# Layer 1's vector sums in other PSUM banks, and another order of splits, norms and squares at three joints of a two-layer backbone

## The chip, the cores and the metric

One core of a Trainium2 chip runs the kernel. The metric is the device time of one execution in microseconds (us); before and after are compared by the medians of several executions. The engines are TensorE (PE, matrix products; PEld is its weight load), VectorE (DVE), ScalarE (ACT), GpSimd (POOL) and SyncE (SP), whose queue issues the transfers here. Each engine works through its own instructions in order and waits on semaphores for the others. PSUM, into which PE writes, has 8 banks of 512 columns.

## The reference, cut to what matters

Two layers over 1024 latent tokens and 256 context tokens of width 1024. Layer 0 mixes tokens by windowed means, layer 1 by attention (8 query heads, 2 key heads of width 128, keys of latent and context tokens). Both end in a gated FFN of width 2816 with a convolution over three positions. Ahead of each part stand an RMS norm and a shift and scale that come from a vector c.

```python
for i in range(DEPTH):
    sh1, sc1, g1, sh2, sc2, g2 = split(silu_c @ ada_w[i] + ada_b[i], 6)
    h = _modulate(_rmsnorm(x, norm_w[i, 0]), sh1, sc1)
    ...
    y = _pool_mixer(...) if i == 0 else _attention_mixer(...)
    x = x + g1 * y
    x = x + g2 * _conv_ffn(_modulate(_rmsnorm(x, norm_w[i, 1]), sh2, sc2), ...)
# attention: q, k = _rmsnorm(q) * q_gain, _rmsnorm(k) * k_gain; rotary on latent q, k;
# p = softmax(q k^T / sqrt(128)); o = p v
```

## The kernel before, in words

All products are done in three passes: every operand is split into a rounded high half, cast by ACT, and a low half, the difference, by POOL or DVE (`split`, L161; the cast is L162, the difference L163; the three matmuls are L166 to L168). Tokens are in ten tiles of 128, 0 to 7 latent, 8 and 9 context.

**Order.** The head of the kernel (layer 0's mixer and the start of its FFN) is put in order by the framework's planner, by its own costs: the code gives instructions in an order of priority (`on`). Where the FFN's first plain product ends, the kernel switches to the order of the program (L874). From there `play` (L567) walks through a list of PE's pieces with their planned duration (T3 = 0.648 us for three matmuls of 512 columns) and issues every other step when its due time is reached. The attention loop is written out by hand, step by step.

**Head.** `mix_out` (L440) takes a mixer product out of PSUM on DVE (L442) and adds it to the tokens on POOL (L443). `norm2` (L482) multiplies a tile by its reciprocal root mean square, on ACT (L484) or DVE (L486). `turn_h2` (L790) transposes the normed tiles on PE (L794) into banks 1, 3 and 5, and DVE and ACT (L800 to L805) make features of them. Before, tiles 0 to 3 are normed on DVE, as steps due in the first microsecond of the FFN's list.

**Layer 0's down projection.** 22 steps of the context part come first, each with a weight row of 512 KB and 128 KB of units, then seven products of sums. `d0_load` (L939) issues the loads four steps ahead, `d0_split` (L952) splits them. `sums0_acts` (L899) loads two operands, makes four sums on DVE (L589, L592) and stores them; the last two of 22 such sums are done beside the context part, due at its start + 8 and + 23. `ada_load` (L1020) fetches rows of layer 1's modulation weights, at times in the list `at_` (L1298).

**Layer 1's tiles.** For each latent tile: V and K (`project(i, 2)`), transposes of the next tile (`prep_b`, L1141: L1111 and L1119, then a split), Q in two halves, and the turn of K (`turn_k`, L1226, transposes L1229). `shape_qk` (L1172) norms Q or K in three parts: square on ACT (L1180) and reduction on DVE (L1181); reciprocal root (L174 to L178) and multiplications (L1186 on DVE, gain L1189 on POOL for Q and on DVE for K); rotation (`rope_ops`, L1195: L1210 to L1214, POOL or DVE).

**Attention.** A score of one head takes two and a half banks, 0 to 2 or 2 to 4, in turn. `soft_max` (L1368) reads it on DVE (L1371), `soft_exp` on ACT (L1376), `soft_div` takes the reciprocal on DVE (L1380) and divides on POOL (L1381). `turn_p` (L1385) transposes probabilities (L1389) into bank 5 or 6 in turn and splits them; `pv` multiplies into bank 7. Per pair of tile and key head there are 10 steps; scores are made at steps 7, 0, 2 and 5. Beside it POOL adds up modulation vectors 3, 4 and 5 of layer 1; `ada_reduce` (L1056) then sums each over partitions on PE (L1064), copies it (L1066), turns it into columns (`ada_cols`, L1047: L323, L1051), and sends the last one out as a row (`to_row`, L302: L305). Its banks before are those of `turn_p`, 5 and 6.

Of the kernel before, what the change touches and what calls it, by code (L numbers as in the profile page):

```python
# [20 lines left out]
KT = D // P  # L21
# [61 lines left out]
def backbone(ctx: ExitStack, tc: tile.TileContext, io, out: bass.AP):  # L83
# [77 lines left out]
    def split(hi, lo, src, lo_eng=None):  # L161
        nc.scalar.copy(hi, src)  # L162
        (lo_eng or nc.gpsimd).tensor_tensor(out=lo, in0=src, in1=hi.bitcast(F32), op=ALU.subtract)  # L163
# [22 lines left out]
    def on(t, *fns):  # L186

        for fn in fns:
            todo.append((t, len(todo), fn))
# [171 lines left out]
    def rstd_of(a, b):  # L361
        rstd_from(ss[:, a:b], D, mm_[:, a:b], rs[:, a:b], tt_[:, a:b])
# [119 lines left out]
    def norm2(i, on_act=False):  # L482
        if on_act:
            nc.scalar.activation(xh2[i], tm(i), AF.Copy, scale=rs[:, i : i + 1])  # L484
        else:
            nc.vector.tensor_scalar(out=xh2[i], in0=tm(i), scalar1=rs[:, i : i + 1], scalar2=None, op0=ALU.mult)  # L486
# [60 lines left out]
    on(71.5, lambda: rstd_of(8, 10))  # L547
    on(71.6, lambda: norm2(8, True), lambda: norm2(9, True))
    on(73, lambda: rstd_of(0, 4))

    h2 = {0: (at(0, KT, 512, r=True), at(16, KT, 512, r=True)),

# [316 lines left out]
    order += [(last, p) for p in (1, 6, 2, "Ga", "Gb", 5, 7, "Va", "Vb", 3, 4)]  # L869
    for j, p in order:  # L870
        put(step0(j, p), j, p)
    acts = [(0.1 + 0.3 * i, lambda i=i: norm2(i)) for i in range(4)] + [(1, lambda: rstd_of(4, NLT))] + [(2, lambda i=i: norm2(i, i > 5)) for i in range(4, NLT)]

    acts += [(t_man, lambda: ctx.enter_context(tc.manual_schedule()))]  # L874
    acts += [(t_lat + 0.01 * q, lambda q=q: t0_subs(q)) for q in range(HK)]
# [265 lines left out]
    def prep_b(i, hf, pt, on_act=False):  # L1141
        turn_half(i, 1, 0, hf, xh_of(i), xf_, pt, on_act)
        if hf:
            split(*h1s[i % 2], xf_.rearrange("p (k t) -> p k t", k=KT), None if i else nc.vector)

    def prep_items(i, banks, on_act=False):
        return [(0.45, lambda hf=hf: prep_b(i, hf, banks(), on_act)) for hf in range(2)]
# [3 lines left out]
    def project(i, cg, bank_=None):  # L1151

        hh, hlo = h1s[i % 2]
        wh, wl = wq[cg]
        qk = qks[i % 2]
        ps = []

        def mm(k):
            if not k:
                ps.append(mmb() if bank_ is None else bank_)  # L1160
            mm3(ps[0], hh[:, k], hlo[:, k], wh[:, k], wl[:, k], k == 0, k == KT - 1)

        def evac():
            if cg < 2:
                nc.scalar.copy(qk[:, 4 * cg : 4 * cg + 4].rearrange("p h d -> p (h d)"), ps[0])
            else:
                nc.scalar.copy(qk[:, HEADS:NH].rearrange("p h d -> p (h d)"), ps[0][:, 0:256])
                nc.scalar.copy(vlat[:, i] if i < NLT else vc[:, i - NLT], ps[0][:, 256:512])

        return [(T3, lambda k=k: mm(k)) for k in range(KT)] + [(0, evac)]  # L1170
# [48 lines left out]
    def turn_q(i, banks, halves=(0, 1)):  # L1219
        for hf in halves:  # L1220
            pt = banks()
            for q in range(4):
                nc.tensor.transpose(pt[:, q * P : (q + 1) * P], qks[i % 2][:, 4 * hf + q], ident)
            nc.scalar.copy(tm(i, hf * 512, (hf + 1) * 512), pt)

    def turn_k(i, pt=None):  # L1226
        pt = tp() if pt is None else pt
        for q in range(KVH):
            nc.tensor.transpose(pt[:, q * P : (q + 1) * P], qks[i % 2][:, HEADS + q], ident)  # L1229
        kv_ = pt[:, 0 : KVH * P].rearrange("p (h t) -> p h t", h=KVH)  # L1230
        split(kth[:, :, i * P : (i + 1) * P], ktl[:, :, i * P : (i + 1) * P], kv_, nc.vector)

    nc.vector.tensor_scalar(out=gain[:, 0], in0=gain[:, 0], scalar1=HD ** -0.5, scalar2=None, op0=ALU.mult)
    def shape_acts(i, which, *times):
        return [(t, lambda p=p: shape_qk(i, which, p)) for p, t in enumerate(times[: 3 if i < NLT else 2])]
# [54 lines left out]
            (ndone[4] + 0.05 + 2.2 * a, lambda a=a, lo=lo: d0_out(lo, 0, BANKS0[4][a], True)),  # L1290
        ]

    for n, t in ((NJ - 2, base + 8), (NJ - 1, base + 23)):
        acts += sums0_acts(n, t, t + 11, 0.9, t + 15, [at(o, 2, HC) for o in ((96, 100), (104, 144))[n % 2]])

    row1 = at(108, 256)
    t = ndone["ctx"]
    at_ = [t - 34, t - 26, t - 18, t - 10, t - 3, t + 3, t + 7, t + 11] + [ndone[1] - 8 + 6.5 * m for m in range(KT)]  # L1298
    at_ += [ndone[2] - 14 + 2.6 * m for m in range(6)] + [ndone[2] + 6.1 + 2 * m for m in range(2)]
    acts += [(t, lambda n=n: ada_load(n)) for n, t in enumerate(at_)]  # L1300
    for u, n0, t, gap, b in ((0, 0, ndone["ctx"] + 4, 2.9, 0), (1, 2 * KT, ndone[2] + 6, 2, 2)):
# [17 lines left out]
    for i in range(NLT - 1):  # L1319
        body = project(i, 2)  # L1320
        if i > 1:
            body += [(0.9, lambda i=i: turn_q(i - 2, tp))]
        if i == 0:
            body.insert(5, (0.2, lambda: turn_k(8)))
        if i == 1:
            body.insert(5, (0.2, lambda: turn_k(0)))
        body += prep_items(i + 1, tp) + project(i, 0)
        if i == 0:
            body += [(0.2, lambda: turn_k(9))]
        body += project(i, 1)  # L1330
        acts += [(base + 16, lambda i=i: rope_in(i + 1))]
        acts += shape_acts(i, "k", base + (7.5 if i else 5.45), base + 9.5, base + 10)
        if i + 2 < NLT:
            acts += [(base + 7.2, lambda i=i: prep_a(i + 2)), (base + 10.5, lambda i=i: prep_s(i + 2))]
        end = base + span(body)
        acts += shape_acts(i, "q", *(end + 0.1, end + 1.5, end + (13 if i < NLT - 2 else 14)))
        if i:
            body += [(0.2, lambda i=i: turn_k(i))]
        pe += body
        base += span(body)  # L1340
# [74 lines left out]
    TS, TT = 2.5 * T3, 0.44  # L1415
    i7 = NLT - 1
    p70, p71 = project(i7, 0), project(i7, 1, bank(7))
    pe += project(i7, 2) + [(0.9, lambda: turn_q(i7 - 2, ptb))] + p70 + p71[:5] + [(0.2, lambda: turn_k(i7, ptb()))] + p71[5:]
    ahead = [(0, h) for h in range(NHG)] + [(1, 0), (1, 1)]
    for n, e in enumerate(ahead):  # L1420
        t = span(pe) + TS
        pe += [(TS, lambda e=e: score(*e))]
        acts += [(t - 0.1, lambda e=e: soft_max(*e))]
        if n < 5:
            acts += [(t, lambda e=e: soft_exp(*e)), (t + 2.4, lambda e=e: soft_div(*e))]
    acts += shape_acts(i7, "k", base + 5.3, base + 6.5, base + 7)
    acts += [(base + 6, lambda: q_split(0)), (base + 11.5, lambda: q_split(1)), (base + 16.7, lambda: shape_qk(i7, "q", 0))]
    acts += [(base + 18.5, lambda: v_split(8)), (base + 25, lambda: v_split(0, nc.vector)), (base + 27.5, lambda: v_split(2, nc.vector))]
    pe += [(TT, lambda n=n: turn_p(n)) for n in range(LOOK)]
    play(pe, acts)  # L1430
    osp = [hl(96, KT, P), hl(140, KT, P)]
# [21 lines left out]
    def ada_add(n):  # L1453
        nc.gpsimd.tensor_tensor(out=acc_[3], in0=acc_[3], in1=ada_row1(n), op=ALU.add)
        ada_next(n)

    extra = {}
    slots = [n for n in range(NT, NTOT) if n % NT in (4, 8)]
    for n, t in zip(range(ADA0, len(ada_list)), slots):
        u, k = ada_list[n]  # L1460
        extra.setdefault(t, []).append(ada_ops[u][k])
        if k:
            extra.setdefault(t + 1, []).append(lambda n=n: ada_add(n))
        sums = ada_reduce(u) if k == KT - 1 else ()
        for m, fn in enumerate(sums):
            extra.setdefault(t + 5 + 5 * m, []).append(fn)
    wo_at = {2: 0, 4: 1, 6: 2, 8: 3, 10: 4, 13: 5, 14: 6, 15: 7}
    pend = [ahead[5]]
    side = {n: lambda i=i, hf=hf: turn_q(i, ptb, (hf,)) for n, i, hf in ((0, i7 - 1, 0), (1, i7 - 1, 1), (16, i7, 0), (19, i7, 1))}
# [458 lines left out]
```

## Time and profile before

| | us |
|---|---|
| median of 3 executions | 2224.29 |
| lowest, highest | 2222.72, 2227.51 |
| the profiled execution, its own time | 2228.45 |
| its span, first to last instruction | 2226.3 |
| PE busy | 2151.0 |
| DVE, POOL, ACT busy | 1528.4, 1325.5, 1000.1 |

The profile is of one execution. A wait is told by the line that waited and the line that ended the wait. All positions in time are microseconds from the first instruction. The head reaches to about 160 us, layer 0's down projection goes from about 700 to 980, layer 1's tiles from there to about 1155, attention to about 1540, and then come the output projection and layer 1's FFN.

### The profile page before, as it was taken

The page shows a single profiled execution, that of the slowest core. Times are in us where ns is not written, and L with a number is a line of the kernel's source. Part 1 is how long each engine was busy: PE and PEld are TensorE (multiplying, and loading weights), DVE is VectorE, ACT ScalarE, POOL GpSimd, SP SyncE. Part 2 cuts the span into 40 slices and gives each one's busy share as a digit, 9 for nine tenths or more (in the row PEclk, how much of TensorE's full clock was granted, in tenths as well). Part 3 has the DMA queues.
Part 4 walks back from the last instruction along what each step waited for, and adds up shares of the span by engine and source line. Part 5 has one row for each costly group of instructions (what it writes and reads, how often), then busy time and mean ns, then how long its engine had stood idle before and what let it go on. Part 6 is the DMA issues. An engine that isn't in the chain of part 4 may idle for free.

```text
span 2226.3 us, 30135 instructions
## 1 busy us (share of the span) xinstructions
PE 2151.0 (97%) x10972; PEld 1775.5 (80%) x10972; DVE 1528.4 (69%) x2101; ACT 1000.1 (45%) x1585; POOL 1325.5 (60%) x881
## 2 busy tenths in 40 slices
PE   7989999999999999999998999999999999999999
PEld 5768888888888777887877877778878888888887
DVE  5677777777778567587776666646776666667565
ACT  4354333443335443544446656644433343344442
POOL 0344677666763467663346766735477777774655
PEclk9999999999999999999999999999999999999999
DMA  8843445544457978660000212122145555559775
GB/s 322 292 127 116 140 137 166 174 140 138 161 163 266 341 275 298 219 198 13 33 22 13 74 62 72 48 80 91 58 151 191 190 193 188 188 194 330 250 242 181
DMA packets 213926, 363.77 MB, mean 163 GB/s; under 512 B 15106, under 2 KB 114066, under 8 KB 213778
## 3 DMA queue, kind: packets, MB, share of 16 engines
q1 hardware_dynamic: 213778, 361.85, 48.0%
q8 instruction: 86, 1.41, 0.2%
q14 instruction: 62, 0.51, 0.1%
HBM read 271.86 MB, written 89.93 MB: 163 GB/s over the span
## 4 chain that ended last, share of the span: by engine, by line
PE 75%; DVE 10%; ACT 4%; issue 4%; POOL 3%; DMA 3%; SPq 0%; ACTq 0%; POOLq 0%; DVEq 0%
PE psum L166 23%; PE psum L167 23%; PE psum L168 23%; PE psum L1389 2%; POOL a_512r L163 2%; DVE a L1371 1%; DVE a L1214 1%; DVE a_512r L163 1%; PE psum L315 1%; DMA a<-g_d 1%; ACT a L1376 1%; PE psum L396 1%; DVE a L1119 1%; ACT a_512r L162 1%; DVE hs L1181 1%
## 5 line engine op out<-in xcount | busy, mean ns | idle before, releaser
L163 POOL TENSOR_TENSOR a_512r<-a,a_512r 128x512 fp32r<-128x512 f32 x353 | 530.6, 1514 | 366.9 <-ACT a_512r L162 309.7
L162 ACT CAST a_512r<-a 128x512 fp32r<-128x512 f32 x507 | 294.4, 618 | 375.1 <-POOL a L657 158.2
L166 PE MATMUL psum<-a_2048r,a_512r 128*128 128x256 f32 (+1 forms) x1120 | 399.4, 357 | 4.1 <-DVE psum L1630 2.4
L167 PE MATMUL psum<-a_2048r,a_512r 128*128 128x256 f32 (+1 forms) x1120 | 399.0, 356 | 0.0
L168 PE MATMUL psum<-a_2048r,a_512r 128*128 128x256 f32 (+1 forms) x1120 | 398.3, 356 | 0.0
L163 DVE TENSOR_TENSOR a_512r<-a,a_512r 128x512 fp32r<-128x512 f32 x154 | 183.3, 1199 | 109.2 <-ACT a_512r L162 105.0
L166 PE MATMUL psum<-a_512r 128*128 128x512 f32 x616 | 242.2, 393 | 0.0
L166 PEld LDWEIGHTS psum<-a_2048r,a_512r 128*128 128x128 f32 x1120 | 211.8, 189 | 37.0 <-DVE psum L1630 2.8
L167 PE MATMUL psum<-a_512r 128*128 128x512 f32 x616 | 239.9, 389 | 0.4 <-POOL a_512r L163 0.4
L168 PE MATMUL psum<-a_512r 128*128 128x512 f32 x616 | 239.9, 389 | 0.0
L167 PEld LDWEIGHTS psum<-a_2048r,a_512r 128*128 128x128 f32 x1120 | 211.6, 189 | 31.1 <-issue 0.4
L168 PEld LDWEIGHTS psum<-a_2048r,a_512r 128*128 128x128 f32 x1120 | 211.5, 189 | 30.2
L719 DVE SCALAR_TENSOR_TENSOR a<-psum,conv,a 128x255 f32<-128x255 f32 (+1 forms) x176 | 154.4, 881 | 89.5 <-ACT a L714 86.2
L166 PE MATMUL psum<-a_4096r,a_1024r 128*128 128x512 f32 x408 | 162.0, 397 | 0.0
L168 PE MATMUL psum<-a_4096r,a_1024r 128*128 128x512 f32 x408 | 160.1, 392 | 1.2 <-POOL a_1024r L163 1.2
L167 PE MATMUL psum<-a_4096r,a_1024r 128*128 128x512 f32 x408 | 160.0, 392 | 0.0
L1649 DVE SCALAR_TENSOR_TENSOR a<-psum,conv,a 128x1023 f32<-128x1023 f32 x88 | 112.9, 1283 | 58.9 <-ACT a L1641 57.4
L163 DVE TENSOR_TENSOR a_512r<-psum,a_512r 128x512 fp32r<-128x512 f32 x160 | 109.5, 690 | 51.6 <-ACT a_512r L162 50.3
L166 PEld LDWEIGHTS psum<-a_512r 128*128 128x128 f32 x616 | 115.6, 188 | 29.9 <-issue 5.4
L1381 POOL TENSOR_SCALAR a<-a,stt 128x1280 f32<-128x1280 f32 x64 | 85.8, 1341 | 86.9 <-DVE stt L1380 73.4
L162 ACT CAST a_512r<-psum 128x512 fp32r<-128x512 f32 x160 | 92.1, 583 | 100.9 <-PE psum L1389 100.9
L168 PEld LDWEIGHTS psum<-a_512r 128*128 128x128 f32 x616 | 115.6, 188 | 24.4
(256 smaller groups left out, 4758.2 us busy)
## 6 DMA issues: line engine op xcount, KB each, us to landing
a<-in_ada_w_dram SPq DMA_DIRECT2D x96, 512.0 KB, 5.0
a<-in_ffn_w_up_dram SPq DMA_DIRECT2D x88, 512.0 KB, 6.7
a<-in_ffn_w_down_dram SPq DMA_DIRECT2D x66, 512.0 KB, 6.4
g_d<-a SPq DMA_DIRECT2D x44, 512.0 KB, 2.7
tw_d<-a SPq DMA_DIRECT2D x44, 512.0 KB, 4.4
a<-g_d SPq DMA_DIRECT2D x44, 512.0 KB, 6.5
sg_d<-a SPq DMA_DIRECT2D x44, 512.0 KB, 4.4
a<-tw_d SPq DMA_DIRECT2D x88, 256.0 KB, 4.3
```

The lines of the kernel that those rows point to most:

```text
L162: nc.scalar.copy(hi, src)
L163: (lo_eng or nc.gpsimd).tensor_tensor(out=lo, in0=src, in1=hi.bitcast(F32), op=ALU.subtract)
L166: nc.tensor.matmul(ps, lh, rh, start=first, stop=False, skip_group_check=shared)
L167: nc.tensor.matmul(ps, lh, rl, start=False, stop=False, skip_group_check=shared)
L168: nc.tensor.matmul(ps, ll, rh, start=False, stop=last, skip_group_check=shared)
L315: nc.tensor.matmul(ps[32 * j : 32 * j + 32], c_t[:, k, :], wt[:, j * 256 : (j + 1) * 256], start=k == 0, stop=k == KT - 1, tile_position=( ...
L396: nc.tensor.matmul(ps[:, a - o : b - o], tm(i, kt * P, (kt + 1) * P), scaled[i][:, a + sh : b + sh], start=q == 0, stop=q == len(parts) - ...
L719: nc.vector.scalar_tensor_tensor(out=dst[:, lo:hi], in0=src[:, lo + d : hi + d], scalar=cv[:, t, f : f + 1], in1=dst[:, lo:hi], op0=ALU.mu ...
L1119: nc.vector.tensor_scalar(out=o, in0=pt[:, q * P : (q + 1) * P], scalar1=sc, scalar2=sh, op0=ALU.mult, op1=ALU.add)
L1381: nc.gpsimd.tensor_scalar(out=pb, in0=pb, scalar1=s_[:, 2:3], scalar2=1.0, op0=ALU.mult, op1=ALU.mult)
L1389: nc.tensor.transpose(pt[:, h * P : (h + 1) * P], probs[(4 * u + h) % len(probs)][:, k * P : (k + 1) * P], ident)
L1649: nc.vector.scalar_tensor_tensor(out=c[:, lo:hi], in0=psum[:, o + lo + d : o + hi + d], scalar=cv[:, t, f : f + 1], in1=c[:, lo:hi], op0=A ...
```

## The change

1. The norms of tiles 0 to 3 ahead of layer 0's FFN go from DVE to ACT, and in the order of priority right behind their reciprocal root.
2. The low half of tile 1's features at the start of layer 1 is made on DVE instead of POOL.
3. The last of the 22 sums of layer 0 (loads, four DVE steps, stores) is due 15 later, and the first eight loads of modulation rows 9 to 1 later.
4. K's square of tile 1 is due at 5.45 instead of 7.5.
5. The second part of tile 6's q norm is due 11 after its tile instead of 1.5. K's square of tile 7 stands right behind its projection, ahead of the turn of tile 5's q; its other parts are due 0.9 and 1.3 earlier.
6. At the start of attention, the square of tile 7's q stands behind the first soft max instead of before it; the first piece of V's split behind the fifth soft max and behind the reciprocal for the fourth head, instead of before that; the sixth soft max is due 0.6 later.
7. The sums of modulation vectors 3 to 5 are taken at steps 4, 7 and 9 of a pair, in banks 3, 0 and 3, instead of 5 and 10 (and 15) steps behind the last row in banks 5 and 6.

```diff
     on(73, lambda: rstd_of(0, 4))
+    on(73.1, *(lambda i=i: norm2(i, True) for i in range(4)))
...
-    acts = [(0.1 + 0.3 * i, lambda i=i: norm2(i)) for i in range(4)] + [(1, lambda: rstd_of(4, NLT))] + [(2, lambda i=i: norm2(i, i > 5)) for i in range(4, NLT)]
+    acts = [(1, lambda: rstd_of(4, NLT))] + [(2, lambda i=i: norm2(i, i > 5)) for i in range(4, NLT)]
...
-            split(*h1s[i % 2], xf_.rearrange("p (k t) -> p k t", k=KT), None if i else nc.vector)
+            split(*h1s[i % 2], xf_.rearrange("p (k t) -> p k t", k=KT), nc.vector if i < 2 else None)
...
-    for n, t in ((NJ - 2, base + 8), (NJ - 1, base + 23)):
+    for n, t in ((NJ - 2, base + 8), (NJ - 1, base + 38)):
...
-    at_ = [t - 34, t - 26, t - 18, t - 10, t - 3, t + 3, t + 7, t + 11] + [ndone[1] - 8 + 6.5 * m for m in range(KT)]
+    at_ = [t - 25, t - 18, t - 11, t - 4, t, t + 4, t + 8, t + 12] + [ndone[1] - 8 + 6.5 * m for m in range(KT)]
...
-        acts += shape_acts(i, "k", base + (7.5 if i else 5.45), base + 9.5, base + 10)
+        acts += shape_acts(i, "k", base + (7.5 if i > 1 else 5.45), base + 9.5, base + 10)
...
-        acts += shape_acts(i, "q", *(end + 0.1, end + 1.5, end + (13 if i < NLT - 2 else 14)))
+        acts += shape_acts(i, "q", *((end + 0.1, end + 1.5, end + 13) if i < NLT - 2 else (end + 0.1, end + 11, end + 14)))
...
-    pe += project(i7, 2) + [(0.9, lambda: turn_q(i7 - 2, ptb))] + p70 + p71[:5] + [(0.2, lambda: turn_k(i7, ptb()))] + p71[5:]
+    pe += project(i7, 2) + [(0, lambda: shape_qk(i7, "k", 0)), (0.9, lambda: turn_q(i7 - 2, ptb))] + p70 + p71[:5] + [(0.2, lambda: turn_k(i7, ptb()))] + p71[5:]
...
-        acts += [(t - 0.1, lambda e=e: soft_max(*e))]
+        t0_ = t - 0.1 if n == 0 else t0_
+        acts += [(t + (0.5 if n == 5 else -0.1), lambda e=e: soft_max(*e))]
         if n < 5:
-            acts += [(t, lambda e=e: soft_exp(*e)), (t + 2.4, lambda e=e: soft_div(*e))]
-    acts += shape_acts(i7, "k", base + 5.3, base + 6.5, base + 7)
-    acts += [(base + 6, lambda: q_split(0)), (base + 11.5, lambda: q_split(1)), (base + 16.7, lambda: shape_qk(i7, "q", 0))]
-    acts += [(base + 18.5, lambda: v_split(8)), (base + 25, lambda: v_split(0, nc.vector)), (base + 27.5, lambda: v_split(2, nc.vector))]
+            acts += [(t, lambda e=e: soft_exp(*e)), (t + (1.55 if n == 3 else 2.4), lambda e=e: soft_div(*e))]
+        if n == 4:
+            acts += [(t - 0.03, lambda: v_split(0, nc.vector))]
+    acts += [(base + 5.6, lambda: shape_qk(i7, "k", 1)), (base + 5.7, lambda: shape_qk(i7, "k", 2))]
+    acts += [(base + 6, lambda: q_split(0)), (base + 11.5, lambda: q_split(1)), (t0_ + 0.01, lambda: shape_qk(i7, "q", 0))]
+    acts += [(base + 18.5, lambda: v_split(8)), (base + 27.5, lambda: v_split(2, nc.vector))]
...
+    REST = {4: 3, 7: 0, 9: 3}
     extra = {}
...
-        sums = ada_reduce(u) if k == KT - 1 else ()
-        for m, fn in enumerate(sums):
-            extra.setdefault(t + 5 + 5 * m, []).append(fn)
+        t += 2
+        for fn in ada_reduce(u) if k == KT - 1 else ():
+            while t % NT not in REST:
+                t += 1
+            extra.setdefault(t, []).append(lambda t=t, fn=fn: (setattr(small, "items", [bank(REST[t % NT])]), fn()))
+            t += 2
```

## Rows read from the trace of the kernel before

**Rows 1.** The page: span, and each engine's busy us, share, instructions.

```profile
span 2226.3 us, 30135 instructions
PE 2151.0 (97%) x10972; PEld 1775.5 (80%) x10972; DVE 1528.4 (69%) x2101; ACT 1000.1 (45%) x1585; POOL 1325.5 (60%) x881
```

**Rows 2.** Waits of PE, whole span: us in total, times, longest.

```profile
PE psum L1389 <- DVE a_512r L163: 5.9, 13, 1.0
PE psum L794 <- DVE a L442: 5.7, 1, 5.7
PE psum L1389 <- DVE mod L1051: 5.7, 3, 2.5
PE psum L1389 <- DVE a L1066: 5.5, 3, 1.9
...
PE psum L1389 <- POOL a L1381: 3.3, 1, 3.3
PE psum L1229 <- DVE st L175: 3.1, 1, 3.1
...
PE psum L166 <- DVE a L1371: 2.3, 5, 1.3
PE psum L1229 <- DVE a L1214: 2.2, 1, 2.2
...
PE psum L166 <- ACT a_1024r L162: 1.9, 1, 1.9
...
PE psum L1389 <- DVE a L305: 1.8, 1, 1.8
...
PE psum L168 <- POOL a_1024r L163: 1.2, 1, 1.2
PE psum L167 <- DVE a_1024r L163: 0.8, 1, 0.8
```

**Rows 3.** Stretches: us, busy us (instructions) of five engines, clock, DMA share, GB/s.

```profile
1286.70:1290.10 3.40, 3.40 (x12) 2.82 (x11) 1.38 (x2) 0.70 (x2) 1.00 (x1) 0.50 0.37 119
1290.10:1293.50 3.40, 3.40 (x22) 2.92 (x21) 2.19 (x3) 1.74 (x2) 0.00 (x0) 1.00 0.09 35
```

**Rows 4.** Timeline of DVE, 103 to 124: start, us, instructions [idle before].

```profile
110.51 5.75 DVE L486 TENSOR_SCALAR a<-a,st 128x1024 f32<-128x1024 f32 x4
...
116.33 2.34 DVE L442 TENSOR_TENSOR a<-psum,a 128x1024 f32<-128x1024 f32 x2
```

**Rows 5.** Timeline of ACT, 103 to 124.

```profile
106.57 2.19 ACT L484 ACTIVATE a<-a,st 128x1024 f32<-128x1024 f32 x2 [1.45 <-DVE st L178]
...
119.16 1.02 ACT L803 ACTIVATE a_2048r<-psum,mod 128x256 fp32r<-128x256 f32 x2 [7.27 <-DVE a L802]
```

**Rows 6.** Timeline of ACT, 726 to 738.

```profile
734.13 0.40 ACT L162 CAST a_256r<-a 128x256 fp32r<-128x256 f32 x1 [7.96 <-DMA a<-g_d]
```

**Rows 7.** A stretch of the down projection, columns as in rows 3.

```profile
726.00:734.00 8.00, 7.61 (x34) 5.98 (x32) 1.23 (x1) 0.17 (x1) 0.00 (x0) 1.00 1.01 372
```

**Rows 8.** Timeline of POOL, 1012 to 1034.

```profile
1013.60 2.37 POOL L163 TENSOR_TENSOR a_1024r<-a,a_1024r 128x1024 fp32r<-128x1024 f32 x1 [7.16 <-ACT a_1024r L162]
...
1032.16 1.29 POOL L1210 TENSOR_TENSOR a<-a,a 128x512 f32<-128x512 f32 x1
```

**Rows 9.** Timeline of DVE in tiles 0 and 1, 1012 to 1037.

```profile
1013.61 2.64 DVE L1189 TENSOR_TENSOR a<-a,gain 128x256 f32<-128x256 f32 x1
...
1027.60 1.04 DVE L1119 TENSOR_SCALAR a<-psum,mod 128x128 f32<-128x128 f32 x3
...
1035.34 1.02 DVE L1214 TENSOR_TENSOR a<-a,a 128x128 f32<-128x128 f32 x4
```

**Rows 10.** Timeline of DVE in tile 7, 1137 to 1158.

```profile
1146.00 4.01 DVE L1214 TENSOR_TENSOR a<-a,a 128x128 f32<-128x128 f32 x4
```

**Rows 11.** Timeline of DVE at the start of attention, 1155 to 1175.

```profile
1155.96 1.22 DVE L1181 TENSOR_REDUCE hs<-a 128x8 f32<-128x1024 f32 x1 [4.28 <-ACT a L1180]
...
1169.54 0.69 DVE L163 TENSOR_TENSOR a_2560r<-a,a_2560r 128x512 fp32r<-128x512 f32 x1 [2.03 <-ACT a_2560r L162]
```

## The prediction

> **What bounds the kernel now.** The first view is the page: TensorE (PE) is busy in 97% of a span of 2226.3 us, and no other engine comes near it [rows 1]. So the time is PE's own work plus the places where PE stands still, and an edit off PE counts only where PE waits for what it touches. The second view is the waits of PE, summed by what ended them [rows 2]. The reader is to see that few single joints carry most of the lost time: 5.7 us at the first transposes of layer 0's FFN (L794), 1.9 and 0.8 in its down projection, 1.2 and 3.1 at the QKV tiles 0 to 2 (L168, L1229), 2.2, 2.3 and 3.3 around the last tile and the start of attention, and 5.5, 5.7 and 1.8 where the transposes of probabilities (L1389) wait for layer 1's vector sums. These are the joints that the diff touches; they add up to 33.5 us. The third view is the granted clock in stretches around them [rows 3]: behind one of the last kind PE works 3.4 us at 0.50 of its clock (1.2 instead of 2.4 GHz) and starts 12 matmuls where the next 3.4 us at full clock have 22. That is 3.4 x (1 - 12/22) = 1.5 us more per such wait. Three more stretches of this pattern lie behind waits that the change aims at: at 737, 1150 and 1457.
>
> **A, norms of tiles 0 to 3 on ScalarE (ACT), at 110 us.** VectorE (DVE) now spends 5.75 us on these four, starting at 110.51 when their reciprocal root is ready, and only then takes the last two gated products out of PSUM (2.34 us) [rows 4]. The transposes use those banks: this is the 5.7. In the change the products start at once, so the banks are free about at 113.0, 5.7 us sooner. The norms cost 2.19 / 2 = 1.1 us each on ACT, which is idle for 7.27 us before its first feature cast at 119.16 [rows 5]. If they start at 110.5, ACT is free at 110.5 + 4 x 1.1 = 114.9, so that the cast comes 4.2 us earlier; if the casts and the square that ACT does there now go first, it comes 3.1 earlier. I take **4.0**. The order in this part is made by the planner, which places anew: bounds -2 (half of the 4.4 us of norms uncovered ahead of the cast) and 5.7.
>
> **B, transfers in layer 0's down projection.** The last sums (two loads of 512 KB, four DVE subtractions and additions, two stores) go 15 us of due time (PE's time at full rate) later, the first eight rows of layer 1's modulation weights up to 9. ACT waits 7.96 us for a tile of the context part, and PE behind it [rows 6]; in that stretch the DMA engines are fully busy (share 1.01, 372 GB/s) [rows 7]. The transfers all stand on SP's queue, and the tile that comes late was queued right behind those moved. Taking 1.5 MB from in front of it is 1.5 / 0.372 = 4.0 us, more than 1.9 + 0.8. It goes: 2.7 + 1.5 of clock = **4.2**. The cover is that the queue has caught up by 15 us later: the bytes come back there, in as full a queue. If they do not fit, the same price is paid later: bounds 0 and 4.2. The modulation rows still have 12 us or more before PE asks for them. On SP they are moved past the loads of some six tiles; DVE's four steps move with them, into the same stream of splits.
>
> **C, the joints of tiles 0 and 1.** The low half of tile 1's features is made by DVE, where as many columns take 2.34 / 2 = 1.2 us [rows 4], instead of GpSimd (POOL), where it takes 2.37 [rows 8]: PE's 1.2 goes. But K of tile 0 stands behind it on DVE and everything after it: +0.2 us. K's square of tile 1 is put ahead of the second half of tile 2's features, whose last move now ends at 1028.64; K's rotation ends at 1036.36, 7.7 us later, and PE has waited 3.1 for it [rows 2, 9]. In tile 0, where the square already stands so early, the multiplication by the gain took 2.64 us from 1013.61, because POOL had started its 2.37 us at 1013.60 [rows 8, 9]. Tile 1 now gets the same sequence, and POOL has a second instruction (1.29) right behind the first [rows 8]. So the chain is: 1.2 to POOL's start, 2.4 + 1.3 on POOL, 1.5 for the rotation = 6.4 us instead of 7.7, less 0.4 for the reduction now in front and 0.2 from tile 0: the end comes 0.7 to **0.9** us sooner, for 4.3 us of waits. The wait mostly moves to one place, and the clock stays down behind it. The bounds are 0.3 and, with no holding, 4.3 + 1.5 = 5.8.
>
> Here the Trainium skill speaks against the edit (SBUF — State Buffer, Who interferes with whom): a DVE instruction with two SBUF inputs and a GpSimd instruction that reads SBUF exclude each other for the whole instruction, and who issues first wins. The two rows of tile 0 agree. By this rule C is worth 0.9, and by DVE's own durations alone it would be 5.8.
>
> **D, last K, sixth q, start of attention.** Tile 6's q norm now stands ahead of tile 7's K on DVE, its gain on POOL; the four rotation steps of K then take 4.01 us beside POOL's rotation of q [rows 10] instead of 1.02 in tile 1 [rows 9]. With K first, K is ready some 3 us before PE comes for it: 2.2 + 1.5 of clock = 3.7. On POOL, q 6 gets behind one q split and ends 3 us later, long before its transposes in attention. Next, the reduction of q 7 (1.22) leaves the place before the first soft max [rows 11] for the one behind it: 0.8 sooner there, but the first exponential waits for it and the next soft maxes for the reciprocals of the first two heads, +0.7: 0.1 left. The half of V that DVE waited 2.03 for and split in 0.69 stood ahead of the reciprocal for the fourth head [rows 11], and PE waited 3.3 for its division on POOL [rows 2]. Placed behind it, about 1.1 of this stays (the reciprocal is still behind a soft max): 2.2. In all **6.0**, bounds 3.5 (only the K) and 7.8 (the low clock behind the 3.3 goes too).
>
> **E, seven sums in banks of resting scores.** Each of three vectors is added up, turned, and one is sent out, until now in the two banks which the transposes of probabilities alternate between; PE, in order, waits for DVE to empty them: 5.5 + 5.7 + 1.8 = 13.0 in seven waits [rows 2]. In the change they use banks of a score whose soft max was issued two or more steps before; nothing else writes these for two steps. PE's and DVE's instructions stay the same in number. All 13.0 go, and two low-clock stretches (at 1286 and 1457), 3.0. I take off 1.1 for the small waits of transposes for splits that the pauses hide (0.4 to 0.5 us each in ordinary units: 5.9 in 13) [rows 2]: **14.9**, bounds 8 (half the waits stay in other form) and 16.
>
> A second rule speaks against this edit (PSUM — Partial Sum Buffer, PSUM bank collisions raise a hardware error): any two engines on one bank must be kept apart, whatever columns they touch, so a sum in a score's bank must wait for its soft max. The trace has that wait (L166 for L1371: 2.3 us in 5, at the start of attention [rows 2]), but none in the loop; by the rule alone seven waits could replace seven.
>
> **Sum.** 4.0 + 4.2 + 0.9 + 6.0 + 14.9 = 30.0 us. The profiled execution took 2228.45 us, 2.1 more than its span: 2198.4 after. It lies 4.2 above the median of the runs, 2224.29, and so I forecast 2224.3 - 30.0 = **2194**.
>
> **Rivals.** (1) The lock does not hold tile 1 (DVE gets in 0.02 us earlier): C is 5.8, time 2189. For it: the distance in rows 8 and 9 is 0.01. (2) The transfers only move: the queue is full throughout, B is 0, 2198. (3) The planner's head: ACT takes the norms in a place where they delay its casts, A between -2 and 0: 2198 to 2200. Against it: 7.27 idle. (4) The sums wait for their new banks, or two of three places do not do what the change says; E is 8: 2201. (5) **Slower than before**: in the sums' new places PE waits for soft max and copy with all later scores behind it. It decides from 1.9 + 30.0 / 7 = 6.2 us for each of the seven, when all the other gains are used up; at 7 us it would be 2230. Against it: the longest of these waits today is 2.5 [rows 2].
>
> **How the numbers follow.** The forecast case 0.55, (1) 0.13, (2) 0.12, (3) 0.11, (4) 0.05, (5) 0.03; 0.01 for gains that cancel to within 0.2%, about what a measurement of this kernel can tell from no change. Cases 1 to 4 are all faster. The range reaches from (1) with the best of D, 2185, to (2), (3) and (4) with half of each other's losses, 2208. Faster 0.96, same 0.01, slower 0.03.
>
> **What would show it.** In the waits of PE after: no L1389 behind L1066, L1051 or L305; no L794 behind L442 over 1.5 us; no wait at 735 in the down projection, and no new one 15 to 25 us later; L168 behind POOL gone, but L1229 in tile 1 still about 3 us behind the rotation, with L1189 near 2.6 us; L1229 of tile 7 without a wait; L1389 behind L1381 near 1 us. I am wrong in kind if PE waits in the loop for L1371 instead, or if the head is not shorter; wrong in size if tile 1's wait closes.

## The result, and the profile after

| | before | after |
|---|---|---|
| median, first comparison (4 and 4 executions), us | 2223.51 | 2195.36 |
| median, second comparison (9 and 5 executions), us | 2224.74 | 2195.03 |
| the profiled execution, us | 2228.45 | 2195.86 |

The ratio is 0.9876 with a 95% interval of 0.9854 to 0.9898, and 0.9868 (0.9850 to 0.9886) in the second comparison. The forecast was 2194, and a gain of 30.0 us; the medians differ by 28.2 and 29.7. A kernel's single executions differ by up to 10.8 us (before, 2218.98 to 2229.74).

The page of after, columns as in rows 1:

```profile
span 2194.1 us, 30131 instructions
PE 2143.0 (98%) x10972; PEld 1770.5 (81%) x10972; DVE 1521.1 (69%) x2098; ACT 1002.2 (46%) x1589; POOL 1323.4 (60%) x880
```

PE has the same 10972 matmuls as before, so they can be laid beside each other one by one. The waits of PE in after, columns as in rows 2 (most line numbers from L547 on are one higher than before):

```profile
PE psum L1390 <- DVE a_512r L163: 6.9, 13, 1.0
PE psum L795 <- ACT a_2048r L804: 6.1, 3, 4.1
...
PE psum L1230 <- DVE st L175: 2.9, 1, 2.9
PE psum L166 <- DVE a L1372: 2.6, 5, 1.3
...
PE psum L1390 <- POOL a L1382: 0.9, 1, 0.9
```

Of the joints in [rows 2], the seven waits for the vector sums, the two in the down projection, the one of tile 0 and the one of tile 7 have no line any more. What is left of the 33.5 us is 2.9 at tile 1, 0.9 at the first division and the waits of scores for soft maxes (L1372), 2.6 now and 2.3 before. At the first transposes PE no longer waits for L442, but 4.1 us for ACT. The line of tile 1 names L175, a small step that DVE has right behind K's rotation; the rotation (L1215) ends 0.14 us before PE goes on, and it is what these transposes need.

**Where the time went.** The table says how many us earlier a matmul of after starts than the matmul of the same number in before, and what was won between two marks (worked out from the start times in the two traces).

| mark, us in before | ahead | won since the mark above | part |
|---|---|---|---|
| 84 | 3.2 | 3.2 | nothing of the change lies here |
| 200 | 5.65 | 2.4 | A |
| 705 | 5.9 | 0.3 | |
| 742 | 10.75 | 4.8 | B |
| 1010 | 10.6 | -0.15 | |
| 1060 | 10.3 | -0.3 | C |
| 1200 | 16.7 | 6.4 | D |
| 1530 | 32.9 | 16.2 | E |
| end | 32.2 | -0.7 | |

The first 3.2 us are no work of the edit. Nor are the 0.7 lost at the end: after has 3.4 us at clock 0.50 from 1597.6 on, and in a second profile of the same kernel (after_again) this stretch is missing and the 0.7 are not lost. Near 27 us, in transfers of modulation weights, PE's clock is at 0.50 (1.2 GHz) for 10.2 us in before and for 3.4 us in after. Windows of before, then of after, columns as in rows 3:

```profile
30.60:34.00 3.40, 3.40 (x18) 2.37 (x19) 0.94 (x2) 0.59 (x1) 0.00 (x0) 0.50 1.02 408
```

```profile
27.50:30.90 3.40, 3.40 (x20) 2.32 (x20) 1.00 (x2) 0.59 (x1) 0.00 (x0) 0.50 1.00 378
30.90:34.30 3.40, 3.40 (x35) 2.44 (x36) 1.61 (x3) 1.17 (x2) 0.00 (x0) 1.00 1.02 413
```

In the experiments below, all alike in this place, this stretch is 0, 3.4, 6.8 or 10.2 us long. So a single time of this kernel says little to some 5 us: a_dve below takes 2194.83 us in its one execution, no more than after, although it is 2.3 us behind in A. All the experiments but c_mid and after_again have one execution each, and they are read from mark to mark instead: "+2.3 in A" means that between the marks of A the kernel falls 2.3 us behind after. (C is read there at 1064 instead of 1060, since part of a gain in tile 1 comes back at a wait between the two.) Where a kernel does not differ from after, such numbers lie within 0.5 of zero (one is 0.8), unless a stretch at clock 0.50 has another length there.

### The profile page after: what moved, and what is told of

It reads as the page before. It is cut to its first block, busy times and chain, and to the rows that moved or that the text cites. A ratio compares the mean times of both kernels' runs of the same rounds, so it can differ in the third digit from the quotient of the medians.

```text
span 2194.1 us, 30131 instructions
## 1 busy us (share of the span) xinstructions
PE 2143.0 (98%) x10972; PEld 1770.5 (81%) x10972; DVE 1521.1 (69%) x2098; ACT 1002.2 (46%) x1589; POOL 1323.4 (60%) x880
## 4 chain that ended last, share of the span: by engine, by line
PE 80%; DVE 8%; ACT 3%; issue 3%; POOL 3%; DMA 2%; SPq 0%; ACTq 0%; POOLq 0%; DVEq 0%
PE psum L166 25%; PE psum L168 25%; PE psum L167 25%; PE psum L1390 3%; POOL a_512r L163 2%; DVE a L1372 1%; PE psum L315 1%; DVE a_512r L163 1%; PE psum L396 1%; DVE a L1215 1%; DVE a L1120 1%; ACT a_512r L162 1%; DVE hs L1182 0%; DMA a<-in_ctx_dram 0%; PE psum L1112 0%
## 5 line engine op out<-in xcount | busy, mean ns | idle before, releaser
L166 PEld LDWEIGHTS psum<-a_512r 128*128 128x128 f32 x616 | 115.6, 188 | 29.9 <-issue 5.8
L168 PEld LDWEIGHTS psum<-a_512r 128*128 128x128 f32 x616 | 115.6, 188 | 24.4
L167 PEld LDWEIGHTS psum<-a_512r 128*128 128x128 f32 x616 | 115.7, 188 | 24.2 <-POOL a_512r L163 1.0
```

What stands on the lines that cost most here:

```text
L166: nc.tensor.matmul(ps, lh, rh, start=first, stop=False, skip_group_check=shared)
L167: nc.tensor.matmul(ps, lh, rl, start=False, stop=False, skip_group_check=shared)
L168: nc.tensor.matmul(ps, ll, rh, start=False, stop=last, skip_group_check=shared)
```

## The experiments

**1. Norms of tiles 0 to 3 back on DVE, or half of them (part A).**

```diff
-    on(73.1, *(lambda i=i: norm2(i, True) for i in range(4)))
+    on(73.1, *(lambda i=i: norm2(i, i < 2) for i in range(4)))
```

This is a_half; in a_dve the line is gone, and the old steps stand in the FFN's list again.

> The new kernel with the norms of tiles 0 to 3 put back on DVE, at their old place. Theory (the head's gain is limited by ACT): measured from the end of the reciprocal root to the first feature cast, the head is as in the kernel before, 8.7 us, against 6.3 us in the new kernel, so that the time is about 2.3 us above the new kernel's; PE waits 5.7 us for L442 again. Rival (the whole 5.4 us by which the new kernel is ahead at 150 us comes from the norms): 5.4 us above. The start of the trace, up to 60 us, where the new kernel was 3.2 us ahead, must then go back too; by the theory it does not belong to the edit and is either way.

> The new kernel with the norms of tiles 0 and 1 on ACT and of 2 and 3 on DVE, both right behind the reciprocal root. Theory: in the new kernel the four norms on ACT (4.3 us) hold up two casts and a square, and the square holds a product buffer, for which DVE's last product waits 4.0 us and the first feature cast with it. With half of them on DVE, ACT is free 2.1 us sooner: PE's 4.1 us wait at 114 shrinks by about 2 us, and DVE's idle time before the last L442 by as much. Rival (DVE's own products are what counts, so that any norm on DVE comes back at its price): two norms of 1.7 us on DVE push the products back, and PE waits 4 us or more.

a_dve: +2.3 in A, and the old wait is back. Waits of PE in a_dve:

```profile
PE psum L794 <- DVE a L442: 5.7, 1, 5.7
...
PE psum L794 <- ACT a_2048r L803: 3.5, 4, 1.4
```

a_half: +0.9 in A. The longest wait for ACT falls from 4.1 to 1.4 us, but 2.4 us of wait for L442 are back. So the edit is worth 2.3 to 2.4. That all four norms belong on ACT is not shown: between these marks a_half has the clock at 0.50 for 13.7 us, after (and a_dve) for 10.2, and 3.4 us less at it were worth 1.3 to 1.4 us in another place (below). Why not the 4.0 of the forecast is seen in the timeline of ACT in after, and in that of DVE:

```profile
107.28 4.27 ACT L484 ACTIVATE a<-a,st 128x1024 f32<-128x1024 f32 x4 [0.70 <-DVE st L178]
111.45 1.12 ACT L162 CAST a_512r<-a 128x512 fp32r<-128x512 f32 x2
112.48 1.05 ACT L356 ACTIVATE a<-a 128x1024 f32<-128x1024 f32 x1
113.44 0.19 ACT L356 ACTIVATION_READ_ACCUMULATOR a<-a 128x1 f32 x1
113.53 0.55 ACT L804 ACTIVATE a_2048r<-psum,mod 128x256 fp32r<-128x256 f32 x1
```

```profile
113.66 1.23 DVE L442 TENSOR_TENSOR a<-psum,a 128x1024 f32<-128x1024 f32 x1 [4.00 <-ACT a L356]
```

The norms start and last as forecast. But two casts and a square now stand between them and the first feature cast, 2.1 us. Before, ACT did these while DVE made the norms, ahead of its idle time; timeline of ACT in before:

```profile
109.71 1.12 ACT L162 CAST a_512r<-a 128x512 fp32r<-128x512 f32 x2
110.74 1.05 ACT L356 ACTIVATE a<-a 128x1024 f32<-128x1024 f32 x1
```

And the last gated product waits 4.0 us on DVE for that square, which writes an unused output into the product's buffer; PE's first transposes go on at 114.13, before this product ends, so it is not what they wait for. Counted from the matmul of L462 that is the mark at 84 (84.21 in before, 80.99 in after), the first feature cast [rows 5] starts 34.95 us behind it in before and 32.54 in after: 2.4 earlier, which is what PE gains.

**2. Only the sums of layer 0 later, the modulation rows at their old times (part B).**

```diff
-    at_ = [t - 25, t - 18, t - 11, t - 4, t, t + 4, t + 8, t + 12] + [ndone[1] - 8 + 6.5 * m for m in range(KT)]
+    at_ = [t - 34, t - 26, t - 18, t - 10, t - 3, t + 3, t + 7, t + 11] + [ndone[1] - 8 + 6.5 * m for m in range(KT)]
```

> Only the last sums of layer 0 (two loads of 512 KB, four DVE steps, stores) stay at their later time; the first eight loads of modulation rows go back to their old times. Theory (each MB in front of the late tile on the queue delays it by 2.7 us at the 372 GB/s of that stretch): the sums' 1 MB is enough for most of the 1.9 + 0.8 us, so that at most 0.5 us of wait and no stretch at clock 0.50 is left at the place, and none comes 15 to 25 us later. Rival (the modulation rows are what stood in front of the tile): at least 1.5 us of wait and the stretch at clock 0.50 stay.

-0.1 in B: the whole gain is there with the sums alone. The stretch of rows 7 in b_sums, and the one behind it:

```profile
726.00:734.00 8.00, 8.00 (x37) 6.60 (x36) 4.77 (x6) 4.09 (x7) 0.00 (x0) 1.00 1.05 391
734.00:742.00 8.00, 8.00 (x37) 6.64 (x36) 5.39 (x7) 4.07 (x6) 0.00 (x0) 1.00 1.01 385
```

PE is busy throughout at full clock. The DMA engines are as full as before: the bytes moved, and PE does not wait where they went. Whether the rows moved alone would have been enough as well was not run.

**3. The joint of tile 1 (part C): a shorter POOL instruction.** POOL makes the low half of tile 2's features for 128 of 1024 columns only; the rest is left out of the computation.

```diff
...
+            if i == 2:
+                nc.scalar.copy(hi, src)
+                nc.gpsimd.tensor_tensor(out=lo[:, 0:1], in0=src[:, 0:1], in1=hi[:, 0:1].bitcast(F32), op=ALU.subtract)
...
```

"The lock" is the name here for what rows 8 and 9 show: a DVE instruction that starts just behind one on POOL lasts about as long as that one (2.64 us beside 2.37; 0.42 alone, below).

> The new kernel, where POOL makes the low half of tile 2's features for the first 128 columns of 1024 only; the other seven eighths of this low half are left out. Theory (the port that DVE and POOL share holds K's gain of tile 1): L1190 falls from 2.67 to about 0.45 us, the first rotation step L1211 from 1.23 to 0.3, and PE's wait of 2.94 us for K of tile 1 goes down to 0.5 us or less; the half clock behind it goes too. In all 2.9 + 1.5 to 3 us less than the new kernel at 1031. Rival (DVE's chain is late by itself, behind the sixth and earlier instructions): the wait stays at 2 us or more.

-3.5 in C, the wait of K is 1.0 us (the expectation said 0.5 or less), and no stretch at clock 0.50 lies behind it. Timelines of after, DVE first and then POOL:

```profile
1019.77 2.67 DVE L1190 TENSOR_TENSOR a<-a,gain 128x256 f32<-128x256 f32 x1
1022.47 1.23 DVE L1211 TENSOR_TENSOR a<-a,a 128x128 f32<-128x128 f32 x1
```

```profile
1019.76 2.40 POOL L163 TENSOR_TENSOR a_1024r<-a,a_1024r 128x1024 fp32r<-128x1024 f32 x1 [1.87 <-issue]
1022.11 1.44 POOL L1211 TENSOR_TENSOR a<-a,a 128x512 f32<-128x512 f32 x1
```

The same multiplication on DVE in c_short_lo2, and POOL's short instruction beside it:

```profile
1021.54 0.42 DVE L1196 TENSOR_TENSOR a<-a,gain 128x256 f32<-128x256 f32 x1
```

```profile
1021.54 0.74 POOL L1149 TENSOR_TENSOR a_1024r<-a,a_1024r 128x128 fp32r<-128x128 f32 x1 [1.90 <-ACT a_1024r L1148]
```

0.42 instead of 2.67 us: the multiplication is held by the 2.40 us on POOL, as the prediction took from tile 0 [rows 8, 9]. Item 2 of the change, the low half of tile 1, was not taken back by itself; that its 1.2 us of wait went is read from the two traces alone.

**4. K's multiplications earlier, the low half of tile 2 on DVE.**

```diff
-            split(*h1s[i % 2], xf_.rearrange("p (k t) -> p k t", k=KT), nc.vector if i < 2 else None)
+            split(*h1s[i % 2], xf_.rearrange("p (k t) -> p k t", k=KT), nc.vector if i < 3 else None)
...
-        acts += shape_acts(i, "k", base + (7.5 if i > 1 else 5.45), base + 9.5, base + 10)
+        acts += shape_acts(i, "k", base + (7.5 if i > 1 else 5.45), base + (5.5 if i == 1 else 9.5), base + 10)
```

> The new kernel with K's multiplications of tile 1 moved ahead of the second half of tile 2's features (due 5.5 instead of 9.5), and tile 2's low half made on DVE. Theory (the lock): K's two multiplications run at 0.43 us each before POOL has anything to do, K is ready about 22 us after the tile's first product instead of 25, and the wait of 2.94 us falls to 0.5 or less; against it stand up to 1.2 us of waiting for the low half of tile 2 at its third matmul: 2 to 4 us better with the clock. Rival (the wait only moves to tile 2's features): L168 waits as long as K did, no gain.

Nothing holds the multiplication (0.42 us), and yet K's wait is longer, 3.6 us. (It is -0.45 in C all the same, since the clock is at 0.50 for 3.4 us behind it instead of 6.8.) Timeline of DVE in c_new:

```profile
1023.52 1.36 DVE L1120 TENSOR_SCALAR a<-psum,mod 128x128 f32<-128x128 f32 x4
1025.99 1.23 DVE L163 TENSOR_TENSOR a_1024r<-a,a_1024r 128x1024 fp32r<-128x1024 f32 x1 [1.11 <-ACT a_1024r L162]
1027.13 0.29 DVE L1211 TENSOR_TENSOR a<-a,a 128x128 f32<-128x128 f32 x1
```

The rotation now stands behind the split, and the split waits 1.11 us for ACT's cast: an engine in order gave back what the lock had cost.

**5. K's square of tile 1 late again; the old order at the start of attention (parts C and D).**

```diff
-        acts += shape_acts(i, "k", base + (7.5 if i > 1 else 5.45), base + 9.5, base + 10)
+        acts += shape_acts(i, "k", base + (7.5 if i else 5.45), base + 9.5, base + 10)
...
-        acts += [(t + (0.5 if n == 5 else -0.1), lambda e=e: soft_max(*e))]
+        acts += [(t - 0.1, lambda e=e: soft_max(*e))]
```

The rest of item 6 of the change is undone with it.

> Two stages go back to their old order, far apart in time: K's square of tile 1 to 7.5, at 1020 us, and the order of soft maxes, squares and V's split at the start of attention, at 1145 to 1175 us. Theory: in tile 1 the transposes of K wait 3 to 3.5 us for the rotation, 0.2 to 0.5 us longer than after (2.9), since the lock gave the early square nearly nothing; at the start of attention L1390 waits 3.3 us for the division L1382 again instead of 0.9, so 2.2 to 2.5 us come back there, with 1.5 us more where the clock falls to 0.50 for 3.4 us longer. Rivals: the early square was worth over 1 us in tile 1 (wait 4 us or more); at the start of attention the order of K and of the sixth q made the gain (wait of L1390 for L1382 under 1.5 us).

Waits of PE in cd_old:

```profile
PE psum L1230 <- DVE st L175: 4.0, 1, 4.0
...
PE psum L1390 <- POOL a L1382: 3.3, 1, 3.3
```

The early square is worth 1.0 us of wait: +0.8 in C. This is the size that the rival gave. In before the wait was only 3.1 with a late square; PE came there 1.0 us later, held at tile 0 [rows 2]. At the start of attention it is +2.7. The wait for the division is 2.4 of this, but the other waits there are 0.9 shorter in cd_old than in after (for soft maxes 2.3 and 2.6, for splits 1.5 and 2.1), and the clock is at 0.50 for 6.8 us instead of 3.4.

**6. The sixth q back in front of the last K (part D).**

```diff
-        acts += shape_acts(i, "q", *((end + 0.1, end + 1.5, end + 13) if i < NLT - 2 else (end + 0.1, end + 11, end + 14)))
+        acts += shape_acts(i, "q", *(end + 0.1, end + 1.5, end + (13 if i < NLT - 2 else 14)))
...
-    acts += [(base + 5.6, lambda: shape_qk(i7, "k", 1)), (base + 5.7, lambda: shape_qk(i7, "k", 2))]
+    acts += shape_acts(i7, "k", base + 5.3, base + 6.5, base + 7)
```

K's square leaves PE's list with it.

> The norm of tile 6's q goes back in front of tile 7's K, and K's parts to their old places; all else is as after. Theory: DVE's four rotation steps of tile 7's K take about 4 us beside POOL's rotation of q again, PE's transposes of K wait 2.2 us, with 3.4 us at clock 0.50 behind them: 3.7 us between 1041 and 1160. Rival (the new order behind it, with the soft max and the squares, made the gain there): no wait of L1230 over 0.5 us, and under 1 us.

+4.0 between 1125 and 1141 (positions in after), the longer time at clock 0.50 included. The rotation of tile 7's K on DVE in d_k, and PE's wait for it:

```profile
1138.58 4.01 DVE L1215 TENSOR_TENSOR a<-a,a 128x128 f32<-128x128 f32 x4
```

```profile
PE psum L1230 <- DVE a L1215: 2.2, 1, 2.2
```

In after the four steps take their own time:

```profile
1132.99 1.02 DVE L1215 TENSOR_TENSOR a<-a,a 128x128 f32<-128x128 f32 x4
```

**7. The sums back in their old banks at their old steps, and in their old banks at the new steps (part E).**

```diff
-            extra.setdefault(t, []).append(lambda t=t, fn=fn: (setattr(small, "items", [bank(REST[t % NT])]), fn()))
+            extra.setdefault(t, []).append(fn)
```

This is e_pos; in e_old the whole loop is the old one.

> The seven sums go back to their old steps and to banks 5 and 6; everything else is as in the kernel after. Theory (the 15.6 us that PE is ahead by between 1172 and 1475 came from this edit alone): PE waits for L1066, L1051 and L305 seven times again, 12 to 13 us in all, two stretches of 3.4 us at clock 0.50 come back, and the distance between the start of attention's loop and its end is 14 to 16 us longer than in the kernel after. Rival (part of it came from the new order at the start of attention, which shifted every later step): less than 10 us come back.

> The sums are taken at the new steps 4, 7 and 9, but in banks 5 and 6, which the transposes of probabilities alternate between. Theory (the bank is what PE waited for): the waits of L1390 for L1066, L1051 and L305 come back in full size, 10 to 13 us in seven, as in the version with the old steps. Rival (the step decides, because DVE has less in front of the copy there): under 4 us of waits.

e_old: +16.0 in E, with seven waits of 13.0 us. Waits of PE in e_old:

```profile
PE psum L1390 <- DVE mod L1052: 5.7, 3, 2.5
...
PE psum L1390 <- DVE a L1067: 5.5, 3, 2.0
...
PE psum L1390 <- DVE a L305: 1.8, 1, 1.8
```

e_pos: +11.3, with 8.0 us in five waits and two stretches at clock 0.50. Theory and rival of e_pos both missed the form of it: with one exception it is not the transposes that wait for the sums, but the sums for the transposes' bank. Waits of PE in e_pos:

```profile
PE psum L1065 <- DVE a_512r L163: 5.9, 3, 2.1
...
PE psum L1390 <- DVE a L305: 1.4, 1, 1.4
...
PE psum L323 <- DVE a_512r L163: 0.7, 1, 0.7
```

The sum (L1065) is queued behind a batch of transposes in the same bank and stands until DVE has split that (DVE starts it at 1268.43 in e_pos; PE goes on at 1269.27). The new steps alone save 16.0 - 11.3 = 4.7 us, the banks, at these steps, 11.3. The new banks at the old steps were not run; and the steps of this test were chosen for other banks, so it is no best case of the old ones.

**8. A new order for two joints.** In ac the norms 2 and 3 go to DVE, the squares of tiles 5 and 6 write elsewhere, and tile 1 gets the order of c_mid; c_mid has that order alone.

```diff
-        square(i, xh2[7 if i == 4 else i], True)
+        square(i, xh2[7 if i in (4, 5, 6) else i], True)
...
+            if i == 2:
+                shape_qk(1, "k", 2)
-            split(*h1s[i % 2], xf_.rearrange("p (k t) -> p k t", k=KT), nc.vector if i < 2 else None)
+            split(*h1s[i % 2], xf_.rearrange("p (k t) -> p k t", k=KT), nc.vector if i < 3 else None)
```

The first edit is in ac alone, with the line on the norms of a_half; K's multiplications stand at 5.5 in both.

> Two stages get a new order. First stage, 105 to 120 us: norms 0 and 1 stay on ACT, 2 and 3 go to DVE, and the squares of tiles 5 and 6 write their unused output into another buffer, so that the last gated product (L442) has no square to wait for. Theory (what is left of the 4.1 us wait of PE is ACT's own work ahead of its first feature cast: norms, two casts, squares): L442 loses its 4.0 us wait, but the cast comes only 0.3 to 0.8 us earlier, since ACT has two squares in front of it now, and PE still waits 3 to 4 us. Rival (PE waits for the banks that L442 empties): under 1.5 us of wait. Second stage, tile 1 at 1020 us: K's multiplications stand ahead of the second half of tile 2's features, its rotation ahead of the low half of them, which DVE makes, so that POOL has no instruction of 2.4 us there. Theory (the lock is what kept K late): the transposes of K wait 1.0 to 1.6 us instead of 2.9, and the product of tile 2 (L168) at most 0.7. Rival (K is late because DVE has too much to do in front of it): 2.5 us or more in the two together.

> The kernel after with the new order in tile 1 alone: K's multiplications ahead of the second half of tile 2's features, K's rotation ahead of their low half, which DVE makes. Theory (the lock kept K late): the transposes of K wait 1.3 us instead of 2.9, nothing waits for the low half, and from the start of tile 1 to the turn of tile 2 PE gains 1 to 2.5 us on the kernel after, by how long the clock stays at 0.50 there; the whole time is 1 to 3 us below that kernel's. Rival (the time comes back at the next joint, where the features of tile 3 now wait for work that DVE did not have before): under 0.5 us at 1060, the same time as after.

> The changed kernel once more, unchanged, beside the run before it: a time of 2194 to 2198 us, and at the start of the trace a stretch at clock 0.50 of another length than in the first profile (there 3.4 us; 0 to 10.2 us in the other kernels), with everything from the mark at L462 on as in the first profile, but for the length of the stretch at 0.50 behind the wait of K in tile 1 (3.4 or 6.8 us).

The head in ac: +1.7 in A. L442 lost its wait for the square, as both theories had it, and neither was right about PE, which waits 2.4 us for L442 at 112 and 3.1 for L804 at 120. Splitting the norms puts L442 behind 2.4 us of them on DVE. By the timelines the 3.1 go back to the lock: DVE's low half of a feature (L806, 0.76 us in after) takes 2.46 us beside an addition on POOL, and the next feature waits behind it. Timelines of ac, DVE and then POOL:

```profile
116.94 2.46 DVE L806 TENSOR_TENSOR a_2048r<-a,a_2048r 128x256 fp32r<-128x256 f32 x1 [1.21 <-ACT a_2048r L804]
```

```profile
116.77 2.35 POOL L443 TENSOR_TENSOR a<-a,a 128x1024 f32<-128x1024 f32 x1
```

The same pair is in a_half (2.47 us at 119.25). What would shorten this joint is still open.

Tile 1: -2.1 in C in both. Timeline of DVE in c_mid, and the wait of PE:

```profile
1017.83 0.43 DVE L1192 TENSOR_TENSOR a<-a,gain 128x256 f32<-128x256 f32 x1
1018.17 1.36 DVE L1120 TENSOR_SCALAR a<-psum,mod 128x128 f32<-128x128 f32 x4
...
1019.97 1.02 DVE L1217 TENSOR_TENSOR a<-a,a 128x128 f32<-128x128 f32 x4
1020.90 1.22 DVE L163 TENSOR_TENSOR a_1024r<-a,a_1024r 128x1024 fp32r<-128x1024 f32 x1
```

```profile
PE psum L1232 <- DVE a L1217: 1.3, 1, 1.3
```

K's rotation fills the time in which the split waited for ACT's cast, K is 1.6 us less late, and PE's clock does not fall there. The rival of c_mid is right in part: the transposes of the next features wait 3.0 us for ACT (L1112 behind L1227, 1.2 at the longest), 1.3 in after. The median of c_mid is 2191.50 us in 4 executions (2190.84 to 2195.20), against 2195.03 of after beside it in 5 (2193.03 to 2196.88): 3.5 us lower, with ranges that still overlap. Its ratio to before is 0.9856 (0.9838 to 0.9875). It has the lowest median here; the 2.1 us in tile 1 are what its trace accounts for. Another 2.1 of its profiled execution is the start, where it happens to have no stretch at clock 0.50.

after_again ran as expected but for the start, where the stretch is again 3.4 us long: from mark to mark up to 1530 it lies within 0.2 us of after, and behind K's wait the clock is at 0.50 for 6.8 us again.

## Why the prediction was right, and where it was not

The sum was 30.0 us; the traces give 32.2 - 3.2 = 29.0, and the medians 28.2 and 29.7. The mechanism was right in B, D and E, which are most of the gain. A was priced too high, and C's gain was lost to a longer stretch of low clock.

- **A, 4.0 forecast, 2.4 measured.** The step that failed is the choice between the two orders on ACT: I put the norms first and counted the cast at their end, 4.2 earlier, without the casts and the square that then come behind them (2.1 us). That work does not vanish when it gives up its place in the idle time. That both products would start at once also failed: the last waited 4.0 us for a buffer, of which the rows before gave no sign.
- **B, 4.2 forecast, 4.8 measured.** The mechanism is right, and the sums are enough for it: 3.2 were won around the two waits, listed as 2.7, and 1.6 in the stretch of low clock, forecast 1.5. The pricing by 1.5 MB took in the modulation rows, whose move changed nothing measurable once the sums were moved. The rival in which the transfers only move fell.
- **C, 0.9 forecast, -0.3 measured.** The two waits fell from 1.2 + 3.1 to 2.9, by 1.4, in the order of the 0.9; the lock held tile 1 (2.67 us beside 2.40), and the first rival, 2189, fell. What I took as fixed was the low clock behind the wait: 3.4 us in before, 6.8 in after, and this took the gain back. In the three kernels with the same wait and 3.4 us behind it, C is 1.0 to 1.1. What sets the length of the stretch no run shows (below).
- **D, 6.0 forecast, 6.4 measured.** K and the sixth q are the 3.7 forecast and 4.0 in d_k, clock included; the start of attention is 2.3 forecast and 2.7 in cd_old. The wait for L1382 is 0.9 now, forecast 1.1. That the total fits so well is partly luck: the waits between these marks fell by 3.9, not 4.5, because small ones grew, and the time at clock 0.50 fell by two stretches of 3.4 us (10.2 to 3.4), where the forecast counted one.
- **E, 14.9 forecast, 16.2 measured** (16.0 by e_old). All seven waits went, both stretches of low clock too; the small waits for splits rose by only 0.6 between these marks (4.2 to 4.8; 1.0 in the whole span), forecast 1.1. The other 0.8 above the forecast stands in no wait that the profile lists. No wait for a soft max took their place in the loop, so the rivals on this side, the slower one too, fell: the sums found their banks free.

The sum held, with some luck, although two of its terms were too high by 1.6 and 1.2, since the other three were too low by 2.3 in all; the stretches between the parts lost 0.5. The number 2194 came from the median of before; from the profiled execution the sum gave 2198.4, and the profiled after took 2195.86: the 3.2 us of the start more than cover the 1.0 that the parts lack. The 2.3 us of waits for L1371, counted in the 33.5, had no term and did not go. The low end of the range, 2185, does not come out of the cases that it names ((1) with the best of D gives 2187.6); the measured time lies inside either way.

## What to carry to other kernels

Where PE alternates between two banks that another engine must empty, a rare extra product in one of them stopped everything queued behind it, with both choices of steps that were tried (13.0 us in seven waits, 8.0 in five); in banks at rest for two steps it met no wait. When work moves to an engine that seemed idle, list what that engine does just ahead of its idle time and which buffers that work holds: the moved work can push it behind itself, and that is what part of the gain was lost to here. Compare kernels that differ by 1% from mark to mark in two traces, since a stretch that nobody touched can differ by more than a part of the change is worth.

## What the runs showed of the hardware

- **The low clock behind a wait varies where order and wait are the same.** K's wait in tile 1 is 2.9 to 3.0 us in eight runs with the same order there. Behind it the clock is at 0.50 for 6.8 us in four of them (both of after, e_pos, a_half), 3.4 in three (e_old, b_sums, a_dve) and not at all in one (d_k). The first is after, the second d_k:

```profile
1024.20:1027.60 3.40, 2.50 (x7) 2.14 (x8) 3.23 (x12) 1.89 (x3) 0.00 (x0) 0.50 0.00 0
1027.60:1031.00 3.40, 3.40 (x9) 2.63 (x9) 2.50 (x5) 1.55 (x3) 0.00 (x0) 0.50 0.45 173
```

```profile
1024.60:1028.00 3.40, 1.74 (x8) 1.13 (x6) 3.37 (x3) 0.56 (x3) 3.15 (x2) 1.00 0.01 2
1028.00:1031.40 3.40, 2.10 (x10) 1.79 (x11) 3.19 (x13) 1.49 (x2) 0.00 (x0) 1.00 0.00 0
```

  One such stretch less is 1.3 to 1.4 us of gain in C (e_old, b_sums, a_dve); by the forecast's estimate it was 1.5.
- **The lock holds tiny DVE instructions as well.** In after, the last step of the reciprocal root of tiles 0 to 3, 4 elements in each partition, takes 2.40 us beside an addition on POOL; the same step for two tiles took 0.16 us a moment earlier. Timelines of DVE, then POOL:

```profile
103.15 0.16 DVE L178 SCALAR_TENSOR_TENSOR st<-st 128x2 f32<-128x2 f32 x1
...
104.84 2.40 DVE L178 SCALAR_TENSOR_TENSOR st<-st 128x4 f32<-128x4 f32 x1
```

```profile
104.82 2.41 POOL L443 TENSOR_TENSOR a<-a,a 128x1024 f32<-128x1024 f32 x1 [1.91 <-DVE st L177]
```

  All norms start behind it. In d_k a TENSOR_SCALAR of 2 elements with one tensor as input (L174) takes 2.21 us beside POOL's 2.40 at 1133. The Trainium skill (SBUF — State Buffer, Who interferes with whom) counts `tensor_scalar` among the operations that can take the shared port and says that who issues first holds it for the whole instruction. The row of d_k agrees with both, and the row of after, a step with two tensors as inputs, with the second: POOL had started 0.02 us earlier. Whether the joint of A gets shorter when this step is kept clear of POOL was not tried.
